# Seven block products for the down projection too, in a transformer layer that is one kernel

## The chip, the core and the metric

One core of a Trainium2 chip runs the whole layer as one launch. The metric is the time of one execution on the device in microseconds (us). Engines: PE is TensorE (matmul), DVE VectorE, ACT ScalarE, POOL GpSimd, SP the queue that issues the DMAs.

## What is computed

One layer of an encoder, x of 2048 tokens by 1024 features, f32:

```python
mixed = concat(neighbourhood attention, latent attention (MLA), gated convolution), normed per 64-wide head
x  = x + g1 * (mixed @ w_out)            # 1024 x 1024
h2 = rms_norm(x) * a2 + b2
gt, up = split(h2 @ w_gu)                # 1024 x 5632
x  = x + g2 * ((silu(gt) * up) @ w_down) # 2816 x 1024
```

g1, g2, a2 and b2 are rows of 1024 that come from a conditioning vector.

## The kernel before

Every f32 matmul is made of three passes: an operand is split into a high part (rounded to fp32r by ACT, `whl[:, 0]`) and the rest (a subtraction on DVE, `whl[:, 1]`), and PE does high x high, high x low and low x high. So each weight or activation tile that comes from DRAM costs one ACT copy (L1302) and one DVE subtraction (L1303) ahead of its matmuls.

The program runs in stages. After the input projections and neighbourhood attention comes **MLA**: 32 units (8 heads x 4 blocks of 512 queries). In each unit PE makes scores (L1178 to L1180), a running maximum for a later unit (matmul L846, DVE reduction L847) and the product with v (L1133); the softmax sums are added half on POOL (L1192) and half on DVE (L1193). `finish` (L1136) copies the result, whose two 64-row halves have still to be added, and stores one half to `mixT` and the other to `mixU`.

Then the tail of the layer, with tokens in four chunks of 512 (two pairs):

- **Output projection** (`out_proj`, L1398), chunk by chunk in two halves of 512 columns, eight steps of 12 matmuls each. `dw_load` (L1028) loads two 128-row blocks of w_out and POOL multiplies them by the gate g1 (L1034). Beside it runs `mix_in` of the next chunk (L1038: loads `mixT` and, for four of its eight tiles, `mixU`, adds them in L1069, norms, splits), and `norm2` (L1423) of the chunk before: it loads x1 from DRAM, squares, scales (L1440), transposes on PE (L1449), modulates on ACT (L1451) and stores to `h2d`. Beside chunk 3, `operands_early` (L1476) loads `h2d` of chunks 0 and 1 and builds five of the operands of the first pair.
- **Gate/up** for a pair of chunks (`gate_up`, L1535), 11 rounds. A round multiplies h2 of the pair by 2 x 256 columns of w_gu. As a 2 x 2 block product (token halves, feature halves, column halves) it takes seven products, not eight (Strassen's scheme in Winograd's form): on the left A11, S2, A12, S3, S1, A22, S4 (built once for a pair), on the right B11, T2, B21, T3, T1, T4, B22 (`gate_prep`, L1321, POOL L1328). Each is 12 matmuls. The four results of a round are stored to `actd`.
- **Down projection** of the pair (`down`, L1564): for each chunk and each half of the columns, 22 steps of 12 matmuls over 2816 rows of w_down (gated by g2 on POOL, L1034) and the stored activations. For pair 0, `norm2` of chunks 2 and 3 and then `operands_early` of pair 1 run beside it; `operands_late` (A22, S4) runs at the head of each gate/up.

Order: PE and SP run in the order written (`manual_schedule`, L1586); in MLA also ACT, DVE and POOL. Elsewhere a scheduler that simulates the program fixes the order of ACT, DVE and POOL at build time. `unit_next` (L1368) hands out split tiles, loads up to three cost units ahead (`AHEAD`) into four buffers of 512 KB (`draw`) and keeps four split tiles ahead. `step(side)` advances the work beside a matmul loop by one yield. Stores are collected in `pending` and issued by `stores()`.

```python
def down(c, half, side, n_side=1):                       # L1564
    ps = [bank() for _ in range(NTT)]                    # 4 PSUM banks
    for f0 in range(0, NFF, 2):                          # 22 blocks of rows
        for e in range(2):
            w, a = unit_next(), unit_next()
            for t in range(NTT):                         # 4 x 3 matmuls
                three(ps[t], a[:, 0, sl], a[:, 1, sl], w[:, 0], w[:, 1], ...)
            step(side, n_side)
```

Of the kernel before, what the change touches and what calls it, by code (L numbers as in the profile page):

```python
# [78 lines left out]
def encoder_trunk(ctx: ExitStack, tc: tile.TileContext, x, cols, pos, inv, rg, ind, sel, b_ada, w_ada, w_adat, crow, w_in, w_conv3,  # L79
# [12 lines left out]
    mixU = scratch([MH * HD, T], "mixU")  # L92
# [718 lines left out]
    with ExitStack() as c3:  # L811
# [194 lines left out]
        xnp = c5.enter_context(tc.tile_pool(name="xnp", bufs=1, reuse_waits="tile"))  # L1006
# [21 lines left out]
        def dw_load(w, gb, row0, n, half, k0):  # L1028

            hs = slice(half * CH, (half + 1) * CH)  # L1030
            kk = min(2, n - k0)
            raw = dwr.tile([P, 2, CH], F32, name="draw")
            dma(raw[:, :kk], w[row0 + k0 * P:row0 + (k0 + kk) * P, hs].rearrange("(k p) n -> p k n", p=P))
            g.tensor_tensor(out=raw[:, :kk], in0=raw[:, :kk], in1=gb[:, None, hs].broadcast_to([P, kk, CH]),  # L1034
                            op=ALU.mult)
            return raw, kk

        def mix_in(c, pool, bank, res, adders, per, bper):  # L1038
# [6 lines left out]
            lat = xnp.tile([P, NTT, CH], F32, name="xn")  # L1045
            halves = lambda ap: ap.rearrange("(f p) n -> p f n", p=P)

            def load(f0):
                f1 = f0 + 2
                dma(mh_[:, f0:f1].bitcast(F32), halves(mixT[f0 * P:f1 * P, csl]))  # L1050
                if 2 <= f0 < 6:
                    dma(lat[:, f0 - 2:f1 - 2], halves(mixU[(f0 - 2) * P:(f1 - 2) * P, csl]))
# [13 lines left out]
            for i, f in enumerate(order):  # L1066
                raw = mh_[:, f].bitcast(F32)
                if 2 <= f < 6:
                    adders[f % 2].tensor_tensor(out=lat[:, f - 2], in0=raw, in1=lat[:, f - 2], op=ALU.add)  # L1069
                    raw = lat[:, f - 2]  # L1070
# [126 lines left out]
        state = {}  # L1197
        m4 = None
        nslots = len(mla) * NP
        with tc.manual_schedule(engines={ET.PE, ET.Activation, ET.DVE, ET.Pool}):  # L1200
            for n in range(0, nslots + 6, 2):
# [33 lines left out]
                if u:  # L1235
# [23 lines left out]
                if ui == len(mla) - 1 and kp == 2 and u:  # L1259
                    pre = [dw_load(w_out, g1b, 0, KD, 0, k0) for k0 in (0, 2)]  # L1260
# [8 lines left out]
    KH = KD // 2  # L1269
    mq = lambda name, bufs, **kw: c4.enter_context(tc.tile_pool(name=name, bufs=bufs, reuse_waits="tile", side="right", **kw))  # L1270
# [8 lines left out]
    actd = scratch([FF, T], "actd")  # L1279

    def split2(src, n=2):

        out = []
        for e in range(n):
            w = wsp.tile([P, 2, CH], F32R, name="whl")
            s.activation(w[:, 0], src[:, e], AF.Copy)
            v.tensor_tensor(out=w[:, 1], in0=src[:, e], in1=w[:, 0].bitcast(F32), op=ALU.subtract)
            out.append(w)
        return out
# [16 lines left out]
    def rows_of(w, gb, row0, n, half):  # L1306
        for k0 in range(0, n, 2):
            item(1, partial(dw_load, w, gb, row0, n, half, k0), unit_split, min(2, n - k0))


    ORDER = ("B11", "T2", "B21", "T3", "T1", "T4", "B22")

    def gate_load(f, u):
        raws = []
        for kh in range(2):
            raw = dwr.tile([P, KH, 2 * P], F32, name="draw")
            dma(raw, w_gu[kh * KH * P:(kh + 1) * KH * P, u * FF + f * P:u * FF + (f + 2) * P].rearrange("(k p) n -> p k n", p=P))
# [28 lines left out]
    def act_load(ff, c):  # L1346
        raw = dwr.tile([P, 2, CH], F32, name="draw")
        dma(raw, actd[ff * P:(ff + 2) * P, c * CH:(c + 1) * CH].rearrange("(k p) n -> p k n", p=P))
        return raw, 2

    for c in range(NCH):
        for half in range(2):
            rows_of(w_out, g1b, 0, KD, half)
    for p in range(PAIRS):
        for f in range(0, NFF, 2):
            for u in range(2):
                item(2, partial(gate_load, f, u), gate_prep, 7)
        for c in (2 * p, 2 * p + 1):
            for half in range(2):
                for ff in range(0, NFF, 2):  # L1360
                    item(1, partial(dw_load, w_down, g2b, ff * P, 2, half, 0), unit_split, 0)
                    item(1, partial(act_load, ff, c), unit_split, 0)
                    i = len(stream)
                    units.extend((i - 2 + k, e) for e in range(2) for k in range(2))
# [25 lines left out]

    def three(ps, th, tl, wh, wl, first, last):
# [4 lines left out]


    def out_proj(c, lhs, side):  # L1398
        for half in range(2):
# [3 lines left out]
            for k in range(KD):  # L1403
                w = unit_next()
                if k == 2:
                    for t in range(NTT):
                        xx = xsp.tile([P, CH], F32, name="xs")
                        dma(xx, x[c * CH + t * P:c * CH + (t + 1) * P, hs])
# [10 lines left out]
        for gen in side:  # L1419
            for _ in gen:  # L1420
                pass

    def norm2(c, name):  # L1423

        yield
        yield
        x1 = blk.tile([P, NTT, D], F32, name=name)
        for t in range(NTT):
            dma(x1[:, t], x1d[c * CH + t * P:c * CH + (t + 1) * P, :])
        yield  # L1430
        ss = small.tile([P, NTT, 2], F32, name="ss3")
        for hf in range(2):
            for t in range(NTT):
# [271 lines left out]
```

## Time and profile before

| | us |
|---|---|
| median of 3 runs (2 others: 3242.45, 3245.36) | 3244.28 |
| the profiled execution, own time | 3238.45 |
| its span, first to last instruction | 3236.7 |

The profile is of one execution. "Idle before ... <-" names what ended an engine's wait. Matmuls are pipelined, so their listed lengths overlap, and the rate is read from their number in a stretch. PEclk is the granted TensorE clock as a share of 2.4 GHz; the lower level is 1.2 GHz.

### The profile page before, as it was taken

How to read it: one execution, taken by the hardware profiler on the slowest of the kernel's cores; microseconds unless marked ns; L12 is line 12 of the kernel's file. 1: busy time of each engine (PE TensorE's matmuls, PEld its weight loads, DVE VectorE, ACT ScalarE, POOL GpSimd, SP SyncE). 2: the span in 40 equal slices, each digit the busy share in tenths (PEclk: the TensorE clock that was granted, in tenths of full speed). 3: DMA queues.
4: the chain of work that ended last, by engine and by line, in shares of the span. 5: the costliest groups of instructions: out<-in, count | busy, mean ns of one | idle time of the engine just before them, and what ended most of it. 6: DMA issues, size and time to landing. Idle time of an engine off the chain costs nothing.

```text
span 3236.7 us, 39081 instructions
## 1 busy us (share of the span) xinstructions
PE 3032.9 (94%) x13818; PEld 2273.7 (70%) x13818; DVE 2049.8 (63%) x2827; ACT 1308.1 (40%) x2286; POOL 1442.3 (45%) x979
## 2 busy tenths in 40 slices
PE   6988999899999999998987999999969899999999
PEld 5877878666555555554655788887747688888777
DVE  7778675556766766766566644446676744445666
ACT  4544444464444344345243333333443333333343
POOL 4424243234454544546455643343454544343443
PEclk9999999999999999999998999999989999999999
DMA  6567465875221222201566322223665422222665
GB/s 217 170 211 246 160 207 142 255 195 142 59 56 30 53 56 59 56 18 59 188 223 200 125 78 79 85 88 130 232 213 195 159 82 85 90 86 92 202 220 196
DMA packets 269638, 440.19 MB, mean 136 GB/s; under 512 B 36777, under 2 KB 122073, under 8 KB 266361
## 3 DMA queue, kind: packets, MB, share of 16 engines
q1 hardware_dynamic: 269442, 437.69, 43.5%
q8 instruction: 109, 1.79, 0.2%
q14 instruction: 87, 0.71, 0.1%
HBM read 340.48 MB, written 97.07 MB: 135 GB/s over the span
## 4 chain that ended last, share of the span: by engine, by line
PE 67%; DVE 11%; DMA 10%; issue 4%; POOL 4%; ACT 2%; SPq 2%; DVEq 0%; POOLq 0%; ACTq 0%
PE bk L1507 8%; PE bk L1508 8%; PE bk L1509 8%; PE op L1133 7%; PE ps L846 4%; PE st L1178 4%; PE st L1179 4%; PE st L1180 4%; DVE whl L1303 3%; PE bk L1395 3%; PE bk L1394 3%; PE bk L1393 3%; POOL draw L1034 2%; PE mm L316 2%; DMA draw<-actd 2%
## 5 line engine op out<-in xcount | busy, mean ns | idle before, releaser
L1303 DVE TENSOR_TENSOR whl<-draw,whl 128x512 fp32r<-128x512 f32 x416 | 407.5, 1024 | 225.6 <-ACT whl L1302 223.8
L847 DVE TENSOR_REDUCE mx<-ps 128x1 f32<-128x1024 f32 x256 | 312.8, 1222 | 226.0 <-PE ps L846 226.0
L1185 ACT ACTIVATE p<-st 128x1024 f32<-128x1024 f32 x256 | 262.0, 1024 | 392.6 <-PE st L1180 375.3
L1302 ACT ACTIVATE whl<-draw 128x512 fp32r<-128x512 f32 x416 | 240.9, 626 | 397.0 <-POOL draw L1034 202.8
L1034 POOL TENSOR_TENSOR draw<-draw,g2b 128x1024 f32<-128x1024 f32 x88 | 228.9, 2601 | 317.5 <-DMA draw<-in_w_down 192.5
L1192 POOL TENSOR_TENSOR acc<-acc,p 128x512 f32<-128x512 f32 x192 | 259.0, 1349 | 158.9 <-ACT p L1185 156.2
L1393 PE MATMUL bk<-whl 128*128 128x512 f32 x704 | 282.2, 401 | 28.2 <-ACT whl L1302 28.1
L1395 PE MATMUL bk<-whl 128*128 128x512 f32 x704 | 283.8, 403 | 18.4 <-DVE whl L1303 17.9
L1394 PE MATMUL bk<-whl 128*128 128x512 f32 x704 | 278.8, 396 | 2.8 <-DVE whl L1303 2.8
L1133 PE MATMUL op<-p,vt 128*64 128x512 f32 x1024 | 248.2, 605 | 0.1
L1328 POOL TENSOR_TENSOR t<-draw,t 128x512 f32<-128x512 f32 x88 | 122.6, 1394 | 235.1 <-DMA draw<-in_w_gu 178.0
L1342 ACT ACTIVATE whl<-t 128x512 fp32r<-128x512 f32 x176 | 111.4, 634 | 284.0 <-PE bk L1509 245.7
L1507 PE MATMUL bk<-q,whl 128*128 128x512 f32 x528 | 207.4, 393 | 13.6 <-DVE ev L1518 10.1
L1508 PE MATMUL bk<-q,whl 128*128 128x512 f32 x528 | 206.9, 392 | 0.0
L1178 PE MATMUL st<-qh,kh 97*128 97x512 f32 x512 | 206.8, 404 | 0.0
L1509 PE MATMUL bk<-q,whl 128*128 128x512 f32 x528 | 205.8, 390 | 0.0
L1179 PE MATMUL st<-ql,kh 96*128 96x512 f32 x512 | 203.1, 397 | 0.0
L1180 PE MATMUL st<-qh,kl 96*128 96x512 f32 x512 | 201.5, 394 | 0.0
L262 POOL TENSOR_TENSOR wlo<-raw,whi 128x768 fp32r<-128x768 f32 (+4 forms) x59 | 112.5, 1906 | 196.0 <-ACT whi L261 176.5
L1193 DVE TENSOR_TENSOR acc<-acc,p 128x512 f32<-128x512 f32 x192 | 190.2, 991 | 3.1 <-ACT p L1185 3.0
L1343 DVE TENSOR_TENSOR whl<-draw,whl 128x512 fp32r<-128x512 f32 x132 | 117.4, 890 | 108.6 <-ACT whl L1342 107.5
L1343 DVE TENSOR_TENSOR whl<-t,whl 128x512 fp32r<-128x512 f32 x176 | 145.6, 828 | 60.9 <-ACT whl L1342 55.2
(339 smaller groups left out, 7283.6 us busy)
## 6 DMA issues: line engine op xcount, KB each, us to landing
draw<-in_w_gu SPq DMA_DIRECT2D x88, 512.0 KB
draw<-in_w_down SPq DMA_DIRECT2D x88, 512.0 KB
draw<-actd SPq DMA_DIRECT2D x88, 512.0 KB
actd<-ev SPq DMA_DIRECT2D x88, 256.0 KB
wt<-in_w_adat SPq DMA_DIRECT2D x32, 512.0 KB
draw<-in_w_out SPq DMA_DIRECT2D x32, 512.0 KB
raw<-in_w_conv SPq DMA_DIRECT2D x32, 384.0 KB
xx<-in_x SPq DMA_DIRECT2D x16, 512.0 KB
```

What stands on the lines that cost most here:

```text
L847: v.reduce_max(mx[:, t, i:i + 1], ps.rearrange("p a b -> p (a b)"), axis=AX.X)
L1133: pe.matmul(tl["op"][e * HD:(e + 1) * HD], vt[:, 2 * kp + e], tl["p"][kp][:, e], start=kp == 0, stop=kp == NP - 1, skip_group_check=True)
L1178: pe.matmul(st[:, e], kh[:, ks], qh[:, qsl], start=True, stop=False)
L1179: pe.matmul(st[:, e], kh[:QKD, ks], ql[:, qsl], start=False, stop=False)
L1180: pe.matmul(st[:, e], kl[:, ks], qh[:QKD, qsl], start=False, stop=True)
L1303: v.tensor_tensor(out=w[:, 1], in0=raw[:, e], in1=w[:, 0].bitcast(F32), op=ALU.subtract)
L1393: pe.matmul(ps, th, wh, start=first, stop=False, skip_group_check=True)
L1394: pe.matmul(ps, th, wl, start=False, stop=False, skip_group_check=True)
L1395: pe.matmul(ps, tl, wh, start=False, stop=last, skip_group_check=True)
L1507: pe.matmul(ps, w[:, 0, k], th, start=first and k == 0, stop=False, skip_group_check=True)
L1508: pe.matmul(ps, w[:, 0, k], tl, start=False, stop=False, skip_group_check=True)
L1509: pe.matmul(ps, w[:, 1, k], th, start=False, stop=k == KH - 1, skip_group_check=True)
```

## The change

1. The down projection of a pair is also one 2 x 2 block product with seven products: 11 steps of 12 matmuls each, 77 steps for a pair in place of 88. Left operands are the activations, right ones blocks of w_down; `actd` now holds seven blocks per round, four of them sums or differences made at the end of `gate_up` (three on DVE, one on POOL). The sums and differences of w_down (T1 to T4) are made beside MLA by `wd_combos`: 44 loads of 256 KB, 44 POOL subtractions, 44 stores to `wdt`.
2. w_out and w_down are no longer multiplied by g1 and g2 when loaded. DVE multiplies the result in PSUM (or in SBUF) by the gate, and POOL adds it to x.
3. `finish` moves the second half of an MLA result across partitions by DMA, and POOL adds the halves (`join`), so `mixU` and its addition go.
4. Chunks 0 and 1 keep x1 in SBUF: their `norm2` reads it there, h stays in SBUF, and the operands of pair 0 are made from it (`first_early` beside chunk 3, `first_late` at the head of gate/up).
5. `norm2` of chunks 2 and 3 becomes `norm2_later`, in 16 pieces beside gate/up of pair 0; their squares are taken in `out_proj`. `operands` of pair 1 is spread over 52 of the 77 steps of the first down projection.
6. Columns of a gate/up round are now one block from each half of the 2816, so a load of w_gu is two DMAs with 512-byte rows, not one with 1024. `ev` has 10 buffers, not 12, and is opened anew for each pair.

Core of the diff:

```diff
-            dma(mixT[256 + h * HD:256 + (h + 1) * HD, qsl], o[:HD])
-            dma(mixU[h * HD:(h + 1) * HD, qsl], o[HD:])
+            tl["o"] = o, mo.tile([HD, CH], F32, name="o2")
+            dma(tl["o"][1], o[HD:])
+        def join(u, tl):
+            g.tensor_tensor(out=o2, in0=o2, in1=o[:HD], op=ALU.add)
+            dma(mixT[256 + h * HD:256 + (h + 1) * HD, qc * CH:(qc + 1) * CH], o2)
...
+                if n >= 16 and n % 4 == 0:
+                    next(combos, None)
+                if prev and kp == 2:
+                    join(prev, state[prev])
...
-            g.tensor_tensor(out=raw[:, :kk], in0=raw[:, :kk], in1=gb[:, None, hs].broadcast_to([P, kk, CH]),
-                            op=ALU.mult)
...
+                for i, (o, x0, x1) in enumerate(((b11, b12, b11), (b12, b22, b12), (b22, b22, b11), (b21, b21, b22))):
+                    yield
+                    g.tensor_tensor(out=o, in0=x0, in1=x1, op=ALU.subtract)
+                    r0 = (0, 2, 1, 3)[i] * hr + k * P
+                    dma(wdt[r0:r0 + P, :], o)
...
             for t in range(NTT):
-                v.tensor_tensor(out=xs[t], in0=xs[t], in1=ps[t], op=ALU.add)
-            for t in range(NTT):
-                dma(x1d[c * CH + t * P:c * CH + (t + 1) * P, hs], xs[t])
+                eg = egp.tile([P, CH], F32, name="eg")
+                v.tensor_tensor(out=eg, in0=ps[t], in1=g1b[:, hs], op=ALU.mult)
+                g.tensor_tensor(out=xs[t], in0=xs[t], in1=eg, op=ALU.add)
+                if x1 is None:
+                    s.activation(eg, xs[t], AF.Square, accum_out=ss2[:, (c - 2) * NTT + t, half:half + 1])
+                pending.append((x1d[tokens(c, t), hs], xs[t]))
...
+    def norm2_later():
+                xa = n2.tile([P, CH], F32, name="n2")
+                dma(xa, x1d[tokens(2, i), half * CH:(half + 1) * CH])
+                yield
+                v.tensor_scalar(xa, xa, rs2[:, i:i + 1], None, ALU.mult)
+                yield
+                tp = bank()
+                for j in range(KH):
+                    pe.transpose(out=tp[:, j * P:(j + 1) * P], in_=xa[:, j * P:(j + 1) * P], identity=ident)
...
+    def first_late(S, h0, h1):
+        for k in range(KH):
+            t = tmp()
+            g.tensor_tensor(out=t, in0=h0[:, k], in1=h1[:, k], op=ALU.subtract)
+            put(S, "S3", k, t)
...
+        comb("S3", a11, a21, ALU.subtract, v)
+        t = comb("S1", a21, a22, ALU.add, g)
+        t = comb("S2", t, a11, ALU.subtract, v)
+        out("A12", a12)
+        comb("S4", a12, t, ALU.subtract, v)
...
+    def down(p, side):
+        def prod(ps, first, at=None):
+            for k in range(NK):
+                a, w = unit_next(), unit_next()
+                for t in range(NTT):
+                    three(ps[t], a[:, 0, sl], a[:, 1, sl], w[:, 0], w[:, 1], first and k == 0, k == NK - 1)
+                if k == 4:
+                    stores()
+                if k == 7 and at:
+                        dma(xx, x1d[tokens(2 * p + i, t), j * CH:(j + 1) * CH])
+                step(side)
+        def put_out(i, j, src):
+                v.tensor_tensor(out=e, in0=src[t], in1=gb, op=ALU.mult)
+                g.tensor_tensor(out=xx, in0=xx, in1=e, op=ALU.add)
...
+        prod(a, True)
+            s.activation(p1[t], a[t], AF.Copy)
+        prod(b, True)
+        add(u2, p1, b)
+        prod(a, False, (0, 0))
+        put_out(0, 0, a)
+        prod(b, False)
+        add(u3, p1, b)
+        prod(c, True, (1, 1))
+        add(u3, u3, c)
+        put_out(1, 1, u3)
+        prod(b, False, (1, 0))
+        add(p1, p1, b)
+        put_out(1, 0, p1)
+        prod(c, False, (0, 1))
+        add(u2, u2, c)
+        put_out(0, 1, u2)
```

## Rows read from the trace of the kernel before

**Rows 1.** The page: busy time of each engine over the span.
```profile
PE 3032.9 (94%) x13818; PEld 2273.7 (70%) x13818; DVE 2049.8 (63%) x2827; ACT 1308.1 (40%) x2286; POOL 1442.3 (45%) x979
```
**Rows 2.** Busy by stretch: length, PE, PEld, DVE, ACT, POOL, PEclk, DMA share, GB/s.
```profile
800.00:1480.00 680.00, 680.00 (x2842) 397.14 (x2840) 474.00 (x488) 283.27 (x324) 340.85 (x261) 1.00 0.22 48
...
1536.00:1799.60 263.60, 226.87 (x904) 164.30 (x905) 160.97 (x195) 93.55 (x172) 140.35 (x83) 0.91 0.56 192
1799.60:2230.00 430.40, 426.56 (x1849) 347.57 (x1848) 225.54 (x285) 140.60 (x229) 188.21 (x126) 1.00 0.28 91
2230.00:2540.00 310.00, 267.71 (x1122) 208.15 (x1121) 209.70 (x217) 132.75 (x243) 141.63 (x64) 0.93 0.64 216
2540.00:2978.00 438.00, 426.04 (x1851) 348.03 (x1850) 227.66 (x290) 139.73 (x229) 187.91 (x127) 0.99 0.26 85
2978.00:3237.00 259.00, 247.76 (x1057) 197.44 (x1055) 169.16 (x189) 98.01 (x171) 108.96 (x44) 0.99 0.60 203
2000.00:2100.00 100.00, 100.00 (x437) 81.85 (x437) 47.80 (x65) 32.97 (x55) 40.11 (x28) 1.00 0.27 85
```
**Rows 3.** Waits of PE in the output projection: total, times, longest.
```profile
PE bk L1393 <- ACT whl L1302: 21.2, 3, 8.8
PE bk L1449 <- DVE q L1440: 10.6, 8, 5.5
```
**Rows 4.** Waits of PE in down 0; then in gate/up 1.
```profile
PE bk L1393 <- ACT whl L1302: 25.8, 10, 10.2
PE bk L1395 <- DVE whl L1303: 13.9, 11, 4.9
...
PE bk L1507 <- DVE ev L1518: 10.0, 1, 10.0
```
**Rows 5.** PE in order of time: three small groups of matmuls.
```profile
1551.68 1.05 PE L1063 MATMUL bk<-t,indf 128*16 128x512 f32 x8
1573.71 0.73 PE L1106 MATMUL bk<-rhl,selr 48*128 48x512 f32 x2
2260.32 0.60 PE L1449 MATMUL bk<-ident,m 128*128 128x128 f32 x4
```
**Rows 6.** Groups in down 0, by line: busy, mean ns, idle before.
```profile
L1303 DVE TENSOR_TENSOR whl<-draw,whl 128x512 fp32r<-128x512 f32 x172 | 175.0, 1065 | 87.4 <-ACT whl L1302 86.9
L1034 POOL TENSOR_TENSOR draw<-draw,g2b 128x1024 f32<-128x1024 f32 x42 | 111.4, 2653 | 160.2 <-DMA draw<-in_w_down 81.4 <-DVE whl L1303 75.7 <-DVE m L1440 3.1
L1302 ACT ACTIVATE whl<-draw 128x512 fp32r<-128x512 f32 x171 | 98.3, 625 | 153.6 <-POOL draw L1034 75.8 <-PE bk L1395 40.7 <-DMA draw<-actd 33.4
L1482 POOL TENSOR_TENSOR ev<-ev 128x512 f32<-128x512 f32 x4 | 6.4, 1596 | 3.5 <-DMA ev<-h2d 2.9 <-DVE q L1474 0.6
```
**Rows 7.** A group in the output projection, by line.
```profile
L1034 POOL TENSOR_TENSOR draw<-draw,g1b 128x1024 f32<-128x1024 f32 x28 | 70.1, 2513 | 83.7 <-DMA draw<-in_w_out 80.8 <-DVE whl L1303 2.9
```
**Rows 8.** POOL, then PE, at the start of the output projection.
```profile
1531.89 1.77 POOL L1069 TENSOR_TENSOR xn<-m,xn 128x512 f32<-128x512 f32 x1 [8.62 <-DMA xn<-mixU]
...
1536.11 0.80 PE L1393 MATMUL bk<-whl,th 128*128 128x512 f32 x1 [8.83 <-ACT whl L1302]
```
**Rows 9.** Groups in MLA (800 to 1480 us), by line; then L1193's own durations.
```profile
L847 DVE TENSOR_REDUCE mx<-ps 128x1 f32<-128x1024 f32 x227 | 277.4, 1222 | 202.8 <-PE ps L846 202.8
L1192 POOL TENSOR_TENSOR acc<-acc,p 128x512 f32<-128x512 f32 x172 | 229.5, 1334 | 151.9 <-ACT p L1185 149.7
...
L1193 DVE TENSOR_TENSOR acc<-acc,p x192: 674/681/2875, 771.3 to 1522.1; 128x512 f32<-128x512 f32 x192
L1193 DVE TENSOR_TENSOR acc<-p,p x32: 679/1437/1734, 768.6 to 1500.8; 128x512 f32<-128x512 f32 x32
```
**Rows 10.** A group in gate/up 0, by line.
```profile
L1547 POOL TENSOR_TENSOR ev<-ev 128x512 f32<-128x512 f32 x31 | 54.5, 1761 | 51.4 <-DVE ev L1526 24.8 <-issue 20.5 <-DVE ev L1532 6.1
```
**Rows 11.** The end: the last additions and the last matmul.
```profile
3230.91 2.73 DVE L1583 TENSOR_TENSOR ev<-ev,bk 128x512 f32<-128x512 f32 x4 [2.82 <-PE bk L1395]
...
3232.53 0.39 PE L1395 MATMUL bk<-whl 128*128 128x512 f32 x1
```

More of the change, by code (lines that the diff above doesn't have):

```diff
@@ L1278, in encoder_trunk @@
     h2d = scratch([D, T], "h2d")
[L1279 to L1289, printed above, removed]
+    actd = scratch([PAIRS * 7 * NK * P, CH], "actd")
+    ss2 = small.tile([P, 2 * NTT, 2], F32, name="ss2", bufs=1)
+    rs2 = small.tile([P, 2 * NTT], F32, name="rs2", bufs=1)
     stream, loaded, units, done = [], list(pre), [], []
@@ L1480, in operands_early, with operands @@
+    def operands(p, S):
+        for k in range(KH):
+            a = []
+            for i in range(2):
+                for j in range(2):
+                    t = tmp()
+                    f, c = j * KH + k, 2 * p + i
+                    dma(t, h2d[f * P:(f + 1) * P, c * CH:(c + 1) * CH])
+                    a.append(t)
+            a11, a12, a21, a22 = a
+            for _ in range(4):
+                yield
             put(S, "A11", k, a11)
             put(S, "A12", k, a12)
+            yield
+            put(S, "A22", k, a22)
@@ L1489, in operands_early @@
             yield
-    def operands_late(p, S):
-        for k in range(KH):
-            a22, a12 = block_load(p, 1, 1, k), block_load(p, 0, 1, k)
-            put(S, "A22", k, a22)
-            for e in range(2):
-                g.tensor_tensor(out=a12, in0=a12, in1=S["S2"][:, e, k].bitcast(F32), op=ALU.subtract)
+            put(S, "S2", k, a22)
+            g.tensor_tensor(out=a12, in0=a12, in1=a22, op=ALU.subtract)
+            yield
             put(S, "S4", k, a12)
-    def gate_set(S, after):
+            for _ in range(4):
+                yield
@@ L1530, in gate_set @@
         after(1, 0, p1)
+        step(side)
         prod(c, "S4", False)
@@ L1548, in up @@
             outs[i, j] = sg
-        gate_set(S, gate)
+        gate_set(S, gate, side)
         stores()
-        gate_set(S, up)
-        for (i, j), t in outs.items():
-            rows, csl = slice((f + j) * P, (f + j + 1) * P), slice((2 * p + i) * CH, (2 * p + i + 1) * CH)
-            pending.append((actd[rows, csl], t))
-    pending = []
-    def stores():
-        while pending:
-            dma(*pending.pop(0))
-    def down(c, half, side, n_side=1):
-        hs = slice(half * CH, (half + 1) * CH)
-        ps = [bank() for _ in range(NTT)]
+        gate_set(S, up, side)
@@ new lines, in prod, with add @@
+                step(side)
+        def add(dst, x0, ps):
+            for t in range(NTT):
+                v.tensor_tensor(out=dst[t], in0=x0[t], in1=ps[t], op=ALU.add)
+        def put_out(i, j, src):
+            gb = g2b[:, j * CH:(j + 1) * CH]
+            for t in range(NTT):
+                e = u3[t] if src is a else src[t]
+                v.tensor_tensor(out=e, in0=src[t], in1=gb, op=ALU.mult)
+                xx = xs.pop(0)
+                g.tensor_tensor(out=xx, in0=xx, in1=e, op=ALU.add)
+                pending.append((out[tokens(2 * p + i, t), j * CH:(j + 1) * CH], xx))
@@ L1601, in encoder_trunk @@
-        spare[0] = ev
         for p in range(PAIRS):
-            operands_late(p, S)
-            for f in range(0, NFF, 2):
-                gate_up(p, f, S)
-            last = p == PAIRS - 1
-            if not last:
-                S = {}
-                side = [norm2(2 * p + 2, "m0"), norm2(2 * p + 3, "m1")]
-                down(2 * p, 0, side[:1])
-                down(2 * p, 1, side[1:])
-                side = [operands_early(p + 1, S)]
-                down(2 * p + 1, 0, side)
-                down(2 * p + 1, 1, [])
-            else:
-                for c in (2 * p, 2 * p + 1):
-                    for half in range(2):
-                        down(c, half, [])
@@ L1619, in encoder_trunk @@
-        stores()
+            with ExitStack() as cg:
+                ev = cg.enter_context(tc.tile_pool(name=f"ev{p}", bufs=10, reuse_waits="tile"))
+                side = []
+                if p == 0:
+                    n2 = cg.enter_context(tc.tile_pool(name="n2", bufs=2, reuse_waits="tile"))
+                    side = [norm2_later()]
+                    first_late(S, h0, h1)
+                for f in range(NK):
+                    gate_up(p, f, S, side)
+                drain(side)
@@ L1620, in encoder_trunk @@
+            with ExitStack() as cd:
+                dnp = cd.enter_context(tc.tile_pool(name=f"dn{p}", bufs=1, reuse_waits="tile"))
+                last = p == PAIRS - 1
+                S = {}
+                down(p, [] if last else [operands(p + 1, S)])
+                stores()
     if dbg:
```

246 lines of the change are left out of this document (154 added, 92 removed).

## The prediction, made before the change was run

> **What bounds the kernel now.** I first read the page's busy times: PE is busy for 94% of the span and the next engine, DVE, for 63% [rows 1]. So time goes either when PE has fewer matmuls or when it waits less, and I look stage by stage for which. The table of stretches [rows 2] shows three kinds. In MLA and in both gate/up stages PE is busy nearly all the time (680 of 680 us, 426.6 of 430.4, 426.0 of 438) at a granted clock of 0.99 to 1.00. In the output projection and in down 0 it is idle for 37 and 42 us, and the clock is 0.91 and 0.93: after a wait PE runs part of its matmuls at the 1.2 GHz level. Down 1 does the same matmuls as down 0 in 259 us, not 310.
>
> To see what stages cost beyond their matmuls I need the pace: 437 matmuls in 100 us at clock 1.00 [rows 2], 0.229 us each. Transposes, statistics and broadcasts cost 0.60 us per four, 1.05 per eight and 0.73 per two [rows 5]. Then:
> - output projection: 768 x 0.229 = 175.9, and 6 x 1.05 + 12 x 0.73 + 16 x 0.60 = 24.7 beside them; work 200.6, **loss 63**;
> - down 0: 88 steps x 12 x 0.229 = 241.8, with 16 x 0.60 = 9.6 for transposes; work 251.4, **loss 58.6**;
> - down 1: work 241.8; the last matmul starts at 3232.5 [rows 11] and the span ends at 3236.7, so a tail of 4.2 and a **loss of 13**;
> - gate/up: 1848 x 0.229 = 423; losses of 7 and 15.
>
> The waits say what the losses are. In the output projection and in down 0 PE waits for split weights (21.2 us; 25.8 and 13.9) and for the normed rows of `norm2` (10.6) [rows 3, 4]. Behind the split stands POOL's gating: L1034 takes 2.5 to 2.65 us a pair of blocks, and ACT's split waits 75.8 us for it in down 0; POOL itself waits for the load (80.8 and 81.4 us) [rows 6, 7]. The chain load, gate, split is late where POOL, in order, is held by other work or a burst of loads delays it.
>
> **The change, part by part.**
>
> *Seven products in down.* 77 steps in place of 88: 132 matmuls fewer for a pair, 30.2 us, on the path in both stages. Work is then 924 x 0.229 = 211.6. Per step ACT still splits two tiles (2 x 0.625 us) and DVE two (2 x 1.065 when POOL collides with it) in 2.75 us of PE [rows 6]. New on DVE are 36 additions and multiplications out of PSUM per pair at 0.68 us (2.73 for four [rows 11]), 20 more than now, 14 us. They cost nothing as long as DVE is done one product (11 x 2.75 = 30 us) later, for only then are the banks written again. DVE's sum in down 0 is 154 splits, 36 evictions and 20 operand splits: 210 us at 1.065 per split, 143 at 0.68; the stage has 225. The cover is thin at the upper end. I take the middle, since POOL's 111 us of gating leave and some 32 operations of 1.6 us (51 us) come.
>
> *Gates at eviction.* 42 of L1034 leave down 0 and 28 the output projection, 111 and 70 us of POOL [rows 6, 7], and a link of 2.6 us leaves the feeding chain. What is late next is the load itself. Bytes per step stay the same (512 KB for each split pair), and down 1 is fed at 203 GB/s with only 13 us lost [rows 2].
>
> *Down 0.* `norm2`'s loads leave, and operands of pair 1 come in four bursts of 1 MB some 36 us apart, no longer in adjacent steps. I take the loss that down 1 has now: 211.6 + 13 = 225, **-85**. Best, no loss, -98; worst, the 58.6 stay, 270 us, -40.
>
> *Down 1.* 211.6 + 7/8 of 13 + tail. The tail grows: after the last matmul stand an addition, a multiplication (0.68 each) and four POOL additions at about 1.5 before the store, 10 us where 4.2 were. 233 us, **-26** (-35 to -20).
>
> *Output projection.* Gone are POOL's gating, the read of x1 back for `norm2` of chunks 0 and 1 (behind the 10.6), the round trip through `h2d` beside chunk 3, and `mixU`. Added: 32 DVE multiplications in place of additions, 32 POOL additions at 1.3 to 1.6 us with only two `eg` buffers, so DVE's third multiplication of a half waits for POOL's first addition, with splits queued behind; four split tiles ahead (11 us) hide that. I take a loss of 16, 217 us, **-47**. Bounds: all 63 gone, or only the 10.6.
>
> *Its start.* PE waited 8.8 us for a split that ACT did after squares waiting on L1069, which waited for `mixU` [rows 8]. L1069 goes; the load of `mixT` stays. **-4** (0 to -9).
>
> *Gate/up 0.* The 64 transposes come here: +9.6 on PE, as much as leaves down 0. `first_late` builds four operands at the head: 16 POOL operations of 1.3 to 1.6 us (21 to 26 us) against a need after 6 x 12 x 0.229 = 16.5 us, with T sums of the weights on the same queue. Some run under chunk 3; I take 7 us late, 0 to 25. **+17**. The added stores and the sums on DVE (3 x 0.7 of 39 us a round) are covered by a DVE 52% and DMA 28% busy [rows 2]. Halving the rows of a w_gu load would at worst double the DMA share, to 0.56.
>
> On that load the Trainium skill (DMA: Bandwidth & Descriptors, Specifications) puts the floor for full rate at 512 bytes, where the new rows just lie; by it this term stays nothing, and no run here shows it yet.
>
> *Gate/up 1.* The wait of 10.0 us is for an `ev` buffer held by late stores of down 0 [rows 4]; these stores are now issued at the end of `down`. **-11** (0 to -12).
>
> *MLA.* 44 subtractions and 32 additions on POOL, 76 x 1.33 = 101 us [rows 9], in a stage where POOL is 50% busy. PE does not wait for POOL there. The chain that could reach PE is the maximum: PE needs L847 done, and DVE has additions in between. L847, out of PSUM, keeps its 1.22 us beside POOL; the additions of two SBUF tensors are 0.68 alone and 1.44 where they meet POOL's [rows 9]. DVE waits 202.8 us for PE in this stretch [rows 9], so I put 0, bounds 0 to +101.
>
> Sum: -4 - 47 + 17 - 85 - 11 - 26 = **-156**. The profiled execution took 3238.45, its span 3236.7; 3238.45 - 156 = 3082. The median is 5.8 above that execution: **3088**. The terms' own bounds, not all at one end, give 3050 to 3125.
>
> **Rivals.**
>
> *The feeds stay late* (0.12). If it is loads, not POOL's gating, that hold the splits (POOL's own idle time says DMA [rows 6, 7]), the output projection and down 0 keep their losses: +47 and +45, **3180**. Against it: down 1, with the same gating and the same loads per step, lost 13.
>
> *MLA slows* (0.07). Each of the 76 POOL operations could hold a DVE addition for its whole length, and DVE's delay reach PE. Half of 101 us gives **3138**, all 3189. Against it: the 202.8 us of slack.
>
> The Trainium skill (SBUF — State Buffer, Who interferes with whom) states this as a rule: a VectorE instruction with two SBUF inputs and a GpSimd one that reads SBUF exclude each other for the whole instruction. The 0.68 against 1.44 us agree with it.
>
> *Slower: DVE's queue in gate/up* (0.03). At the end of every round DVE's S2 waits for POOL's S1, and S4 for POOL's product; the splits of the next round stand behind. POOL has three products of 1.76 us queued there [rows 10]. Splits are four tiles, 11 us, ahead, so a round loses only what DVE is held beyond 11 us. To end slower the 22 rounds must lose 166 us, 7.5 each: DVE held 18.5 us a round. Three products and S1 make 7. Price at that point: **3254**.
>
> The change does what it says: the counts are in the code.
>
> **How the numbers follow.** The forecast has 0.76, the rivals 0.12, 0.07 and 0.03; 0.02 is left for mixtures that land near no change. A measurement of this kernel can tell about 0.2% (6.5 us) from nothing. Faster 0.95, same 0.02, slower 0.03. The range goes from the forecast's low end, 3050, up to 3145, to take in half of MLA's rival; the feeds' rival and the slower one stay outside.
>
> **What would show it.** Stretches of about 225 and 233 us for the downs, 217 for the output projection at a clock above 0.95, 447 and 427 for gate/up, MLA unchanged. L1303's successor below 0.95 us in down. Wrong would be: waits of PE on splits with a load as their releaser in down 0 (feeds), PE idle at L846's successor in MLA, or waits at the head of each round.

## The result, and the profile of the changed kernel

| | us |
|---|---|
| before, median of 4 runs beside the change | 3244.82 (3242.45 to 3250.25) |
| changed, median of 4 runs | 3132.47 (3125.90 to 3138.71) |
| ratio, 95% interval | 0.9651 (0.9627 to 0.9675) |
| changed, the profiled execution, its own time and span | 3138.71 and 3136.9 |

The gain is 112 us. The forecast was 156 (3088 us, range 3050 to 3145). The profiled execution is the slowest of the four.

The table of stretches of the changed kernel; the columns are those of [rows 2]. In order: the middle of MLA, output projection, gate/up 0, down 0, gate/up 1, down 1.

```profile
800.00:1480.00 680.00, 664.86 (x2723) 385.78 (x2722) 464.00 (x468) 268.36 (x304) 429.23 (x318) 0.98 0.30 74
1566.00:1774.50 208.50, 205.33 (x904) 155.78 (x904) 135.60 (x175) 95.20 (x185) 98.51 (x71) 0.99 0.49 171
1774.50:2245.60 471.10, 441.24 (x1912) 356.83 (x1913) 294.19 (x350) 172.70 (x315) 233.22 (x153) 0.97 0.37 115
2245.60:2479.70 234.10, 218.53 (x931) 175.11 (x930) 160.94 (x212) 105.03 (x183) 52.38 (x34) 0.99 0.65 218
2479.70:2911.70 432.00, 425.42 (x1845) 347.69 (x1844) 251.91 (x316) 134.95 (x222) 193.71 (x131) 0.99 0.33 104
2911.70:3137.00 225.30, 210.91 (x925) 172.85 (x923) 133.66 (x189) 89.11 (x153) 27.62 (x18) 0.99 0.62 211
```

Against [rows 2] three stages are much shorter (output projection 263.6 to 208.5, down 0 310 to 234, down 1 259 to 225), and their clock is 0.99. Two are longer. MLA lost 119 matmuls in 680 us (2842 to 2723): PE now waits there. Gate/up 0 took 471 where it took 430. (Below, a stage's length runs from its first matmul to the next stage's; so counted, down 0 takes 232.9 us.)

The waits of PE that answer to it (engine, line, releaser: total us, times, longest), in MLA, in the first 55 us of gate/up 0, and in down 0:

```profile
PE mi L1185 <- POOL al L1181: 15.1, 6, 2.8
...
PE bk L1601 <- ACT ev L1608: 16.2, 1, 16.2
PE bk L1601 <- DVE ev L1618: 6.0, 1, 6.0
PE bk L1501 <- DVE n L1497: 3.8, 1, 3.8
...
PE bk L1421 <- DVE whl L1321: 15.6, 15, 4.3
```

The waits of before on splits and on `norm2` [rows 3, 4] are gone from the output projection (5.8 us are left), and in down 0 only DVE's own split is late, 15 times for about 1 us.

**MLA.** The same moment on three engines, each in order of time: SP, POOL, PE (start, us, engine, line, operation; in brackets the idle time before and what ended it):

```profile
867.32 0.45 SPq L831 DMA_DIRECT2D kl<-knl  x1
867.97 0.44 SPq L1056 DMA_DIRECT2D wdt<-wt  x1
868.65 0.49 SPq L1157 DMA_DIRECT2D o<-o  x1
...
881.02 1.27 POOL L1162 TENSOR_TENSOR o<-o,o 64x512 f32<-64x512 f32 x1 [7.14 <-DMA o<-o]
882.26 1.78 POOL L1181 TENSOR_TENSOR al<-acc,ah 128x512 fp32r<-128x512 f32 x1
...
884.09 0.40 PE L1185 MATMUL mi<-al,ones_r 128*1 128x512 f32 x1 [2.20 <-POOL al L1181]
```

The stretch from 868 to 882 us, with the columns of the table above:

```profile
868.00:882.00 14.00, 13.89 (x58) 8.21 (x58) 9.85 (x12) 5.39 (x7) 4.82 (x4) 1.00 1.04 215
```

SP had just issued seven loads of the next head; then it issues the move of half a result across partitions (`o<-o`, 128 KB). The DMA engines are full (share 1.04), and the move lands 12 us later. POOL's `join` (L1162) stands for it in order, and `al` (L1181), which PE needs, stands behind `join`. This happens at six of the seven head changes; POOL waits 45.9 us so in all. PE's own waits for `al` are 15.1 us of the stage's loss; in the 16 us behind this one (882 to 898) the granted clock was 0.89.

In the text of the kernel the move stands at the first double step of a unit and the head's loads at the third. SP is not among the engines whose order is fixed by hand in MLA (L1221 names PE, ACT, DVE and POOL), and the scheduler put the loads ahead. Issuing the move ahead of them was not tried.

**The head of gate/up 0.** ACT from the first split of w_gu to the copy of the first product, then POOL:

```profile
1773.82 0.63 ACT L1360 ACTIVATE whl<-draw 128x512 fp32r<-128x512 f32 x1 [7.03 <-DMA draw<-in_w_gu]
...
1780.83 0.64 ACT L1523 ACTIVATE m<-t 128x512 fp32r<-128x512 f32 x1 [1.06 <-POOL t L1540]
...
1789.31 0.63 ACT L1523 ACTIVATE m<-t 128x512 fp32r<-128x512 f32 x1 [0.95 <-POOL t L1544]
...
1797.13 0.63 ACT L1458 ACTIVATE eg<-xs 128x512 f32<-128x512 f32 x1 [0.94 <-POOL xs L1456]
...
1797.89 0.60 ACT L1608 ACTIVATE ev<-bk 128x512 f32<-128x512 f32 x1
...
1774.78 1.54 POOL L1346 TENSOR_TENSOR t<-draw 128x512 f32<-128x512 f32 x1 [9.27 <-DMA draw<-in_w_gu]
1776.59 1.29 POOL L1346 TENSOR_TENSOR t<-draw,t 128x512 f32<-128x512 f32 x1 [0.27 <-DMA draw<-in_w_gu]
1777.83 6.43 POOL L1540 TENSOR_TENSOR t<-q,q 128x512 f32<-128x512 f32 x4
1784.23 3.38 POOL L1456 TENSOR_TENSOR xs<-xs,eg 128x512 f32<-128x512 f32 x2
1787.57 6.19 POOL L1544 TENSOR_TENSOR t<-q 128x512 f32<-128x512 f32 x4
1793.72 3.38 POOL L1456 TENSOR_TENSOR xs<-xs,eg 128x512 f32<-128x512 f32 x2
```

PE waits 16.2 us for the copy L1608 of a product that it had finished long before. In ACT's fixed order the copy stands behind eight splits (of S3 and S1) and the squares of chunk 3, and each of these waits for one POOL operation. POOL makes 12 of them in one row, 1777.8 to 1797.1, after 9.3 us without work and two sums of weights.

**The end.** The last matmul, the last addition on POOL, the last store; the span ends at 3136.9:

```profile
3126.87 0.39 PE L1422 MATMUL bk<-whl 128*128 128x512 f32 x1
...
3131.25 2.81 POOL L1703 TENSOR_TENSOR xs<-xs,u 128x512 f32<-128x512 f32 x2 [0.68 <-DVE u L1701]
...
3128.64 5.77 SPq L1428 DMA_DIRECT2D out<-xs  x4
```

### The profile page after: what moved, and what is told of

The parts are those of the page before. It is cut to its first block, busy times and chain, and to the rows that moved or that the text cites. A ratio compares the mean times of both kernels' runs of the same rounds, so it can differ in the third digit from the quotient of the medians.

```text
span 3136.9 us, 38944 instructions
## 1 busy us (share of the span) xinstructions
PE 2958.9 (94%) x13554; PEld 2225.1 (71%) x13554; DVE 2031.2 (65%) x2892; ACT 1300.0 (41%) x2298; POOL 1377.5 (44%) x1011
## 4 chain that ended last, share of the span: by engine, by line
PE 66%; DMA 11%; DVE 11%; issue 5%; POOL 3%; ACT 2%; SPq 1%; POOLq 0%; ACTq 0%; DVEq 0%
PE bk L1601 8%; PE bk L1603 8%; PE bk L1602 8%; PE op L1147 7%; PE ps L846 4%; PE bk L1421 3%; PE bk L1420 3%; PE bk L1422 3%; PE st L1198 3%; PE st L1199 3%; PE st L1200 3%; DVE whl L1321 2%; PE mm L316 2%; PE mm L320 2%; PE mm L321 2%
## 5 line engine op out<-in xcount | busy, mean ns | idle before, releaser
L1321 DVE TENSOR_TENSOR whl<-draw,whl 128x512 fp32r<-128x512 f32 x372 | 282.3, 792 | 183.7 <-ACT whl L1320 183.1
L1320 ACT ACTIVATE whl<-draw 128x512 fp32r<-128x512 f32 x372 | 219.3, 625 | 314.0 <-PE bk L1422 193.2
L1421 PE MATMUL bk<-whl 128*128 128x512 f32 x616 | 243.5, 395 | 20.2 <-DVE whl L1321 20.2
L1346 POOL TENSOR_TENSOR t<-draw 128x512 f32<-128x512 f32 x88 | 124.3, 1413 | 273.1 <-DMA draw<-in_w_gu 209.2
L1422 PE MATMUL bk<-whl 128*128 128x512 f32 x616 | 241.0, 391 | 0.0
L1420 PE MATMUL bk<-whl 128*128 128x512 f32 x616 | 240.8, 391 | 0.0
L1601 PE MATMUL bk<-q,whl 128*128 128x512 f32 x528 | 210.7, 399 | 24.5 <-ACT ev L1608 16.2
L1361 DVE TENSOR_TENSOR whl<-t,whl 128x512 fp32r<-128x512 f32 x176 | 171.2, 974 | 62.8 <-ACT whl L1360 58.3
L1602 PE MATMUL bk<-q,whl 128*128 128x512 f32 x528 | 208.6, 395 | 0.0
L1603 PE MATMUL bk<-q,whl 128*128 128x512 f32 x528 | 207.7, 393 | 0.0
L846 PE MATMUL ps<-kh,qh 96*128 96x512 f32 x512 | 179.2, 432 | 3.9 <-DMA kh<-krh 2.1
L320 PE MATMUL mm<-whi,hh 128*128 128x288 f32 (+3 forms) x512 | 171.4, 346 | 8.3 <-ACT hh L384 4.9
```

Of the source, the lines that this page charges most:

```text
L846: pe.matmul(ps[:, e], qs, kh[:QKD, kc:kc + CH], start=True, stop=True)
L1321: v.tensor_tensor(out=w[:, 1], in0=raw[:, e], in1=w[:, 0].bitcast(F32), op=ALU.subtract)
L1420: pe.matmul(ps, th, wh, start=first, stop=False, skip_group_check=True)
L1421: pe.matmul(ps, th, wl, start=False, stop=False, skip_group_check=True)
L1422: pe.matmul(ps, tl, wh, start=False, stop=last, skip_group_check=True)
L1601: pe.matmul(ps, w[:, 0, k], th, start=first and k == 0, stop=False, skip_group_check=True)
```

## The experiments

All ratios are against runs of the kernel before on the same chip, with 95% intervals. Stage lengths come from one profiled execution each.

### MLA: is it the wait of `join`, or POOL's added work?

```diff
-                if prev and kp == 2:
-                    join(prev, state[prev])
                 if prev:
                     for stage, at in enumerate((0, 2, 2, 4, 4)):
...
+                if prev and kp == (6 if u else 4):
+                    join(prev, late.pop(prev))
```

> The join of an MLA result's halves moves from the second to the fourth double step of the next unit, behind the softmax sums in POOL's order; nothing else changes. Theory A (queue order): the added 27 us of MLA are six or seven waits of POOL's join for its transfer at head changes (45.9 us in all), with the sums behind it on POOL and PE's sums behind those (15.1 us of PE waits); then the units at head changes take 23.7 us again as the others do, MLA falls from 780 to 753 to 757 us, and the time to about 3105. Theory B (the transfers themselves: the head's loads share the DMA with 22 MB of new loads and stores of w_down sums): PE still waits at head changes, for other releasers, and MLA stays within 8 us of 780.

Measured: 3106.42 us, ratio 0.9578 (0.9540 to 0.9616). POOL's waits for these moves, in the changed kernel and in this run (total us, times, longest), and the stretch 800 to 1480 us of this run:

```profile
POOL o L1162 <- DMA o<-o: 45.9, 6, 8.3
...
POOL o L1162 <- DMA o<-o: 4.3, 1, 4.3
```

```profile
800.00:1480.00 680.00, 680.00 (x2838) 398.34 (x2840) 483.37 (x486) 280.89 (x321) 451.46 (x333) 1.00 0.31 78
```

From its first product with v to the first matmul of the output projection the stage falls from 788.8 to 765.6 us, and the median falls by 26. POOL is busy even longer (451 us in place of 429), and PE is busy for 680 of 680 us again. So the added POOL work, all 76 operations of it, costs PE nothing; `join`'s place in POOL's queue cost 26 us.

### The head of gate/up 0

*Chunk 3's additions of x on DVE, not POOL* (four POOL operations fewer in the row above):

```diff
-                g.tensor_tensor(out=xs[t], in0=xs[t], in1=eg, op=ALU.add)
+                (v if c == 3 else g).tensor_tensor(out=xs[t], in0=xs[t], in1=eg, op=ALU.add)
```

> In the output projection of chunk 3 the addition of x runs on DVE, not on POOL (8 additions). Theory A (POOL's queue sets the head of gate/up 0): POOL held four of these additions between the first sums of the left operands, ACT's squares and then its copy of the first product stood behind them; the wait of 16.2 us falls to 3 to 8, gate/up 0 from 471 to 455 to 462. Theory B (the sums of left operands themselves are too much for the head: 16 POOL and 20 DVE operations against 16.5 us of matmuls): the wait moves to a later product of the first set and the total wait at the head stays above 22 us of 28.

Measured: 3134.16 us, 0.9659 (0.9627 to 0.9692), the same as the change. Gate/up 0 took 468.1, and the wait for the same copy was 15.7 us. POOL now idled 25.6 us for the first w_gu load and then made the same sums, with waits for DVE's splits between. With the edit of the first experiment as well:

> Both edits above together. If both causes are as named and apart from each other, the gains add: MLA near 755, gate/up 0 near 458, time 3090 to 3097. If the head of gate/up 0 is set by the sums themselves, 3100 to 3107.

Measured: 3107.61 us, 0.9577 (0.9544 to 0.9610), as with the later `join` alone; gate/up 0 took 469.5.

*Sums and splits of S3, S1, A22 and S4 written only where the product that needs them comes* (on top of the later `join`); then also *S3's four sums made beside chunk 3*:

```diff
         def prod(ps, op, first):
+            if at:
+                at(op)            # first round of pair 0: sums and splits of op are made here
...
             put(S, "S2", k, t)
             yield
+        S["s3"] = s3_sums(h0, h1)  # the second run only
+        yield
```

> On top of the later join: the late operands of pair 0 (S3, S1, A22, S4) are traced just ahead of the product that reads each, so that the copy of the first product of gate/up stands ahead of their splits in ACT's order. Theory C (ACT's order): in both kernels so far the copy of the first product stood behind eight splits of S3 and S1, which wait for POOL's sums; with the copy ahead PE no longer waits 16 us there; what is late next is S3 itself (POOL starts its four sums only after the weights' sums, whose load lands late), about 5 to 9 us. Total wait at the head falls from 29 to 12 to 18 us, gate/up 0 from 470 to 452 to 460, time 3090 to 3097. Theory B (too much work for the head): the waits move to S3 to S4 and their total stays above 22.

> As the run before, and POOL's four sums of S3 are traced beside chunk 3, where POOL is idle for 9 us ahead of gate/up (25 us with the additions on DVE). Theory C: S3 is ready when its buffer comes free; the total wait at the head falls to 6 to 14 us, gate/up 0 to 447 to 455, time 3085 to 3093. Theory B: no better than the run before.

Measured: 3104.72 us, 0.9568 (0.9552 to 0.9584), and 3101.75 us, 0.9555 (0.9537 to 0.9572). The first is no more than the later `join`: the copy still waited 21.0 us, since ACT, whose order the scheduler sets and not the text, still had splits and squares ahead of it. The second shortened gate/up 0 from 467 to 456.5 (that wait 9.1 us), but the output projection went from 208.2 to 213.3.

*Both of these and chunk 3's additions on DVE:*

> e3b_head_early with chunk 3's additions after the gate on VectorE instead of GpSimd. Theory A (what is left at the head of gate/up 0 is GpSimd's queue: it makes the sums of the first weight blocks, four S1 sums and the last additions in one row, and the first copy of a product stands behind squares and splits that wait for it): gate/up 0 falls from 456.5 to 444 to 451 us and the median lies 4 to 12 us below 3101.75. Theory B (the first weight loads set it, as in e2, where the same move did nothing): gate/up 0 stays 453 to 460 and the median within 4 us of 3102.

Measured: 3099.26 us, 0.9563 (0.9548 to 0.9579); gate/up 0 took 456.3 and the copy still waited 8.8 us. So it is not enough to take the last additions off POOL: in that trace ACT's last steps before the copy are two squares of chunk 3, which now wait for DVE's additions, and two splits. Moving the squares out of ACT's way was not tried. This version and the one before it have the lowest medians, about 1% under the change; most of that is the later `join`, and their intervals overlap with its own, so here too the stage lengths carry the argument.

### Down and output projection: was it POOL's gating?

*POOL's pass put back on the load path of the changed kernel* (a multiplication by ones: 2.0 to 2.1 us for two blocks, where the gating took 2.5 to 2.65 [rows 6, 7]), for w_out, then for w_down and its combinations:

```diff
             dma(raw[:, :kk], w[...])
+            if w is w_out:                    # second run: if w is w_down or w is wdt
+                g.tensor_tensor(out=raw[:, :kk], in0=raw[:, :kk], in1=ones_f[:, None, 0:1].broadcast_to([P, kk, CH]),
+                                op=ALU.mult)
```

> A multiplication by one on POOL is put back between load and split of w_out (32 of them, 2.5 us each), with the gate still applied at eviction. If POOL's link in the feeding chain was what made the output projection slow before (loss 63 us), most of the 55 us gained there are lost again: 208 becomes 235 to 260. If the gain came from the rows kept in SBUF and the missing round trips through DRAM, it stays at 208 to 218.

> On the changed kernel: a multiplication by one on POOL between load and split of w_down and its sums (84 of them, 2.6 us each for two blocks), gates still applied at eviction. If POOL's link and its collisions with DVE made the down projections slow before (loss 59 and 13 us), down 0 goes from 233 to 255 to 275 and down 1 from 225 to 232 to 240. If the loads set the pace, or norm2's rows and the operands' bursts did, both stay within 5 us.

Measured: 3165.49 us, 0.9754 (0.9721 to 0.9786), output projection 208.4 to 231.0; and 3195.83 us, 0.9845 (0.9825 to 0.9865), down 0 from 232.9 to 269.9 and down 1 from 225.2 to 251.4. In down 0 of the second run the splits, by line, are as in [rows 6], slow on DVE and waiting for POOL on ACT:

```profile
L1324 DVE TENSOR_TENSOR whl<-draw,whl 128x512 fp32r<-128x512 f32 x150 | 148.7, 1031 | 65.0 <-ACT whl L1323 64.5
L1323 ACT ACTIVATE whl<-draw 128x512 fp32r<-128x512 f32 x150 | 87.0, 623 | 129.8 <-POOL draw L1034 79.4 <-PE bk L1425 43.8 <-DMA draw<-actd 4.5
```

So with everything else changed, even this shorter pass costs 23, 37 and 26 us. That is its price on the changed kernel, not what the gating cost before: in down 1 the whole loss before was 13 us.

*The other way round: the kernel before with the gates at eviction and nothing else* (the diff's lines of `out_proj`, and the same in `down`):

> The kernel before with one part of the change alone: w_out and w_down are not multiplied when loaded; DVE multiplies the result by the gate and POOL adds it to x. If the gating was the larger part of the losses: output projection 263 to 230 to 245, down 0 from 310 to 265 to 280, down 1 from 259 to 250 to 255, time 3165 to 3195. If the loads and round trips through DRAM were: output projection and down 0 stay within 12 us, time above 3215.

Measured: 3226.01 us, 0.9940 (0.9921 to 0.9959): 19 us, where the prediction had put POOL's gating behind the losses of both stages. Down 0 took 298.9 and the output projection 267.4. In down 0, ACT's split by line, then SP's waits:

```profile
L1301 ACT ACTIVATE whl<-draw 128x512 fp32r<-128x512 f32 x171 | 98.4, 625 | 144.8 <-PE bk L1394 80.5 <-DMA draw<-actd 60.5 <-PE bk L1510 2.1
```

```profile
SPq L1456 <- ACT t L1452: 47.2, 12, 6.5
```

The split no longer waits for POOL but for a load, 60.5 us. SP issues in the order written here, and it stands 12 times at the `h2d` stores of `norm2` until ACT has made what is stored; the next loads come behind. That gave a new theory: a second limit beside the gating, SP's order. Three runs for it, all on the kernel before: x1d stored at the third step of the next half and `h2d` one step late, with the gates at eviction (e7); the same stores with POOL's gating (e8); and e7 with `h2d` three steps late in down 0 (e10).

```diff
-                    dma(h2d[...], hs[f - 1 + e])
+                    todo.append((f + d, (h2d[...], hs[f - 1 + e])))   # issued d steps on
...
-                dma(x1d[...], xs[t])
+                pending.append((x1d[...], xs[t]))                     # issued at k == 2 of the next half
```

> The kernel before with its gates applied at eviction (as in e6_before_gate_at_eviction) and, besides, with the stores of the second norm moved behind the work that they wait for: x1d is stored at the third step of the next half instead of right after the additions, h2d one step after its two activations. Transfers, bytes and the eight-product down projection stay. Theory A (the second limit of the output projection and of down projection 0 was SP's order: in e6 SP stands 76.8 us for the additions and 55.4 us for the activations of the norm in the output projection, 47.2 us for the activations in down projection 0, with the loads of weights and activations queued behind): down projection 0 falls from 299 to 260 to 272 us, the output projection from 267 to 230 to 250, and the median lies 45 to 75 us below e6's 3226, near 3165. Theory B (it is the amount that is read and written there, and the round trip itself): down projection 0 stays above 290, the output projection above 260, and the median within 12 us of 3226.

> The kernel before with the late stores of e7 alone; POOL's gating of the weights stays on the load path. Theory A (two limits side by side, either of which is enough to hold PE up): the gain alone is small, 10 to 30 us (median 3215 to 3235), with ACT's splits then waiting for POOL's gating in the records, and the gain of e7 is larger than the gains of e6 and of this run added up. Theory C (SP's order alone was the limit and gating only followed it): the median falls by nearly as much as e7's, 3160 to 3190.

> e7_gate_and_late_stores with the h2d stores of the norm of chunks 2 and 3 (those in down projection 0) issued three steps after their activations instead of one; in the output projection they stay one step late. In e7 one step was too little: SP still stood 47.4 us in down projection 0 at these stores, 12 times, and the next load of activations and of weights came directly behind each. Theory A (SP's order is the second limit of down projection 0): SP's waits for the norm's activations there fall under 15 us, ACT's waits for loaded activations (60.6 us in e7) under 30, down projection 0 from 295 to 265 to 282 us, the median from 3208.8 to 3178 to 3196. Theory B (the loads are late for what they move and for the round trip, and SP's wait is only where that shows): down projection 0 stays above 290 and the median within 8 us of 3209.

Measured (one kernel per line; stage lengths in us):

| | gates | stores | output projection | down 0 | median | ratio |
|---|---|---|---|---|---|---|
| before | POOL | at once | 263.5 | 309.9 | 3244.8 | 1 |
| e6 | eviction | at once | 267.4 | 298.9 | 3226.0 | 0.9940 (0.9921 to 0.9959) |
| e8 | POOL | late | 278.4 | 306.1 | 3255.0 | 1.0044 (1.0029 to 1.0059) |
| e7 | eviction | late | 248.6 | 295.4 | 3208.8 | 0.9896 (0.9876 to 0.9915) |
| e10 | eviction | late, `h2d` 3 steps | 248.2 | 285.8 | 3202.1 | 0.9867 (0.9842 to 0.9893) |

Late stores alone made the kernel slower: `norm2` reads x1d later, and in the output projection of e8 PE waited 28.7 us for its rows (10.6 before):

```profile
PE bk L1460 <- DVE q L1445: 28.7, 8, 14.2
```

With the gates gone as well the output projection fell by 19 us against e6. That fits two limits of which either is enough to hold PE, but it is not shown: e8 has this new wait of its own, PE's waits for ACT's splits hardly differ (21.2 us before, 20.6 in e6, 18.4 in e8, 18.6 in e7), and what fell from e6 to e7 are the waits for `norm2`'s rows (17.5 to 12.5) and for a statistic of `mix_in` (5.9 to 0.4). Nor does SP's standing decide by itself. SP's waits at the x1d stores in the output projection of the changed kernel, where PE waits only 5.8 us, then before:

```profile
SPq L1428 <- POOL xs L1456: 60.5, 12, 21.3
SPq L1428 <- POOL q L1456: 32.6, 12, 12.1
...
SPq L1418 <- DVE xs L1416: 91.7, 24, 22.2
```

In down 0 one step was too little for `h2d`: SP still stood 47.4 us in e7. With three steps (e10), in down 0, by line; then SP in order of time; then a stretch:

```profile
L1301 ACT ACTIVATE whl<-draw 128x512 fp32r<-128x512 f32 x172 | 99.4, 626 | 133.1 <-PE bk L1394 103.1 <-DMA draw<-actd 25.5 <-PE bk L1525 4.1
```

```profile
2363.96 9.34 SPq L1482 DMA_DIRECT2D ev<-h2d  x8
2373.40 2.07 SPq L1577 DMA_DIRECT2D out<-ev  x4
...
2377.49 7.78 SPq L1482 DMA_DIRECT2D ev<-h2d  x8
```

```profile
2362.00:2402.00 40.00, 25.42 (x90) 19.29 (x89) 37.50 (x39) 19.96 (x36) 26.65 (x16) 0.78 0.71 221
```

SP's wait at these stores is down to one of 2.1 us, ACT's waits for loaded activations fell from 60.6 us (e7) to 25.5, and down 0 is 10 us shorter. No run has the `h2d` stores late by three steps with POOL's gating in place. The theory's size was missed (265 to 282 was expected), and the medians of e7 and e10 have intervals that overlap, so here the stage lengths carry the argument. What is left of PE's waits in down 0, 14.5 of 24.2 us, lies between 2360 and 2420, where the next pair's operands are made: 16 reads of `h2d` in two adjacent steps, PE at 90 matmuls in 40 us and a granted clock of 0.78. The reads need not be the cause. DVE is busy for 37.5 of these 40 us, and the split that ended PE's longest wait, 8.6 us, stood in ACT's order behind splits of operands that waited for POOL's sums (ACT, then PE):

```profile
2382.51 0.63 ACT L1489 ACTIVATE q<-ev 128x512 fp32r<-128x512 f32 x1 [1.04 <-POOL ev L1503]
2383.05 2.17 ACT L1301 ACTIVATE whl<-draw 128x512 fp32r<-128x512 f32 x4
...
2383.71 0.80 PE L1392 MATMUL bk<-whl 128*128 128x512 f32 x1 [8.62 <-ACT whl L1301]
```

The change removes all three: gates, `norm2` beside down, and operands in adjacent steps. How the rest splits between the reads, the work on operands and fewer loads was not tried.

## Why the prediction was right or wrong

| step | predicted | measured | |
|---|---|---|---|
| start of output projection | -4 | -4.9 | 8.8 [rows 8] to 3.9 us |
| output projection | -47 | -55 | loss 7.7, not 16 |
| gate/up 0 | +17 | +40 | 23 us more than costed; the first 55 us lost 34 |
| down 0 | -85 | -77 | loss 21.3, not 13; 15.6 of it waits for DVE's split |
| gate/up 1 | -11 | -5 | the 10.0 us wait went, 6.6 of others are left |
| down 1 | -26 | -34 | loss past the tail 3.6, not 11 |
| MLA | 0 | +25 | `join` waits for a DMA |

The measured terms, before rounding, sum to -110. Ahead of MLA's first product with v the profiled execution of the changed kernel took 10.0 us more, 6.6 of them in neighbourhood attention, whose length varies between runs (134 to 142 us, counted to that product, in the profiles of all these kernels). So the two profiled spans differ by 99.8 us, and the medians by 112.

That the result lies in the range is in part luck. The terms' own bounds ended at 3125, 7.5 us under the median; the range went on to 3145 for a rival on MLA whose mechanism did not cause the loss there, and it covered MLA and gate/up 0 instead.

**MLA is the step that failed in kind.** The text said "PE does not wait for POOL there" and priced `join` by its 1.33 us. It did not price what `join` waits for. Its bounds, 0 to 101, held the 25 us only by a mechanism that was not the cause. The rival on MLA named that mechanism, each POOL operation holding a DVE addition; in the changed kernel the additions' medians and the maximum are as in [rows 9], and the mean of the first group rose from 962 to 1012 ns in 800 to 1480, 8 us in all (all durations of the line in ns, least, median and most; then the group by line in 800 to 1480 us):

```profile
L1213 DVE TENSOR_TENSOR acc<-acc,p x192: 674/682/1754, 781.1 to 1558.7; 128x512 f32<-128x512 f32 x192
...
L1213 DVE TENSOR_TENSOR acc<-p,p x32: 677/1429/1434, 778.6 to 1538.7; 128x512 f32<-128x512 f32 x32
```

```profile
L847 DVE TENSOR_REDUCE mx<-ps 128x1 f32<-128x1024 f32 x220 | 269.0, 1223 | 216.8 <-PE ps L846 214.3
```

The later `join` gave all of it back. The Trainium skill (SBUF — State Buffer, Who interferes with whom) states that a VectorE instruction with two SBUF inputs contends with a GpSimd one that reads SBUF; the 682 against 1429 ns agree with it. It had no price here: DVE waits 217 us for PE in this stretch.

**Gate/up 0 failed in size.** The "7 us late" took the sums as POOL's work beside PE's first products, needed after six of them; S3 is read by the fourth. And it missed that ACT's copy of the first product and the splits share one fixed order, so a late sum holds a product that is done: one wait of 16.2 us, two of 6.0 and 3.8, and a granted clock of 0.75 over the first 55.5 us, in which PE made 92 matmuls (21 us at the pace of 0.229). Neither the row of POOL operations (four moved to DVE did nothing) nor the order in the text explains it alone; sums made earlier do, in part.

**The gating was only part of the reason.** "Behind the split stands POOL's gating" is true in the trace of before, and putting a shorter pass back on the changed kernel costs 23, 37 and 26 us. But with the gating alone removed the loads were late instead in down 0, as the rival "the feeds stay late" had it: down 0 fell by 11, the output projection not at all. The terms of the output projection and of down 0 came out close because the change also took away other limits: in down 0 SP's stands at the `h2d` stores of `norm2`, worth 10 us between e7 and e10, and the operands in adjacent steps, which no run took out alone. The prediction listed these removals but gave them no price of their own, so the closeness is in part luck. Which removal freed the output projection stays open.

**Right:** seven products (down 1 at 211.6 of work plus a 10.0 us tail, from 3126.87 to 3136.9), splits in the downs under 0.95 us (812 ns in down 0, 758 in down 1, where [rows 6] had 1065), and the covered steps. Its sum of DVE's work in down 0 counts 20 operand splits where there are 28 (L1524), and 12 of its 36 operations "out of PSUM" read only SBUF, at 0.71 to 0.73 us; with 28 the sum is 148 to 218 us, and DVE was busy for 160.9. In the middle of gate/up 1, 300 us hold 1311 matmuls in both kernels, with the added stores, sums and 512-byte rows. Changed kernel, then before:

```profile
2550.00:2850.00 300.00, 300.00 (x1311) 245.81 (x1310) 175.16 (x220) 94.02 (x155) 137.98 (x94) 1.00 0.34 106
```

```profile
2600.00:2900.00 300.00, 300.00 (x1311) 245.80 (x1311) 145.13 (x196) 95.67 (x156) 123.91 (x87) 1.00 0.25 81
```

DMA share per GB/s is about the same (0.25 for 81, 0.34 for 106), so the halved rows cost no rate that shows here. The floor of 512 bytes for full rate that the Trainium skill gives (DMA: Bandwidth & Descriptors, Specifications) agrees with that. The rounds lose nothing, so the slower rival never started.

## What to carry to other kernels

Cost a new operation on an in-order engine by what it waits for as well as by its length, and put it behind the work that others need: moving `join` to a later step of the unit was worth 26 us, and its own length nothing. When a stage waits for a chain, look at every link that could be last, SP's order among them. Removing one of several limits may bring little, and its worth then shows only when the others are gone: the gating alone brought 11 and 0 us in two stages, and a shorter pass put back on the changed kernel cost 37 and 23 there. An eviction that shares an engine's order with preparation for later products can hold the products that are already done.

## What the runs showed of the hardware that was not expected

A 128 KB move within SBUF took 12 us to land while the DMA engines were full with loads issued before it (share 1.04 at 215 GB/s). The same rate took only 0.65 of their time in down 0 (218 GB/s), so per byte the transfers of that stretch, mostly a head's loads, kept the engines busy 1.6 times as long as the transfers of down 0. And where PE was waiting, the clock added to it: 0.78 over the 40 us of operands in e10 and 0.94 over its whole down 0, against 0.99 in the changed kernel's.
